# One core, two hybrid layers: the second layer's gate blocks one by one over both token halves, residual updates tied to low parts, token loads tied to H loads

## The chip, the cores and the metric

The kernel runs on one core of one Trainium2 chip. The metric is the device time of one execution in microseconds. Three executions of the kernel before took 1627.13 us (median), from 1626.03 to 1629.71. A profiled execution comes beside them; all traces below are of that one.

The engines are called as the profile calls them: PE (TensorE, matmuls), PEld (its weight loads), ACT (ScalarE), DVE (VectorE), POOL (GpSimd) and SP (SyncE, which here only issues DMAs; POOL issues some too). Each engine takes its instructions strictly in the order in which they stand in its queue, so an instruction that waits holds up all that stands behind it.

## The reference

Two layers, 512 tokens, width 2048, all in float32:

```python
def hybrid_layer(x, w_in, w_out, g_pre, g_post, w_alpha, b_alpha, g_gla, g_att, rel_bias):
    h = rmsnorm(x, g_pre)
    z = h @ w_in                                   # 2048 x 7184
    gq, gk, gv, gg, ga, aq, ak, av, ag = split_columns(z)
    log_a = jax.nn.log_sigmoid((ga @ w_alpha + b_alpha)) / GLA_TAU
    o_gla = gla_chunk_causal(gq, gk, gv, log_a)    # 4 heads, state carried over chunks of 64
    o_gla = rmsnorm(o_gla, g_gla) * jax.nn.silu(gg)
    o_att = chunk_band_attention(aq, ak, av, rel_bias)   # 8 heads
    o_att = rmsnorm(o_att, g_att) * jax.nn.silu(ag)
    y = jnp.concatenate([o_gla, o_att], axis=-1) @ w_out  # 2048 x 2048
    return x + rmsnorm(y, g_post)
```

Most of the work is the two projections, `h @ w_in` and `... @ w_out`. The change touches the end of the first layer's output projection, the residual sum behind it, and the first blocks of the second layer's input projection: the two attention gate blocks, `silu(ag)`.

## The kernel before

**Blocks, chunks and jobs.** The columns of `w_in` are cut into 14 blocks of 512 and those of `w_out` into 4. A block is read in 8 chunks of 256 rows, each one tile of 128 partitions x (2 x 512) float32, 512 KB. One chunk's use is a *job* (class `Job`, a list `stream` fixes their order). A job has three parts, each on an engine of its own: `load` (a DMA from SP, L151), `high` (ACT rounds the chunk to a reduced format, `wh`, L202), and `low` (DVE takes what the rounding left, `wl = src - wh`, L211). The token operand is split in the same way, and a product is three matmuls: high x high, high x low, low x high. `ahead()` prepares the jobs some three to five places before PE uses them. Raw chunks live in rings of buffers (`raw` 5, `H` 4, `wh` 4, `wl` 3), so a load waits until an old chunk's low part was taken, and a low part until PE has done with the one three jobs back.

**Two kinds of product.** `std_gemm` (matmuls in L311) multiplies one block plainly: 8 jobs, each with 6 matmuls per token tile of 128 (there are 4 token tiles, two per *half*). `fast_gemm` (L389, L379) takes two blocks together and needs seven products, P1 to P7, of four jobs each, instead of eight; it adds or subtracts chunks on DVE first (`H + r`, L196, for P5, P6 and P4; `H - r`, L198, for P7) and uses sums of token operands ("sa") that are stored in DRAM and read back by SP (L178). In a layer's last pair, W23, the jobs run P1 and P2 in turn, then P5 and P6, P3, P7 and P4.

**Between the layers.** When the third product of W23 is done, the first half of the tokens is finished: `finish_both` (L1366 on) sums the squares, POOL takes the power -1/2 (L431), and DVE adds the scaled projection to the tokens `x`, one instruction per piece (L1386: four of 128x1024 for half 0; two of 128x1024 and four of 128x512 for half 1). Each piece is stored to `x_mid`. `prep_half` then makes the next layer's operand of that half: ACT squares the pieces (L444), DVE sums (L445), POOL takes the power, ACT (L499) and DVE (L501) scale, PE transposes in 32 instructions (L515), ACT evicts (L526), and ACT and DVE split into high and low (L105, L106). Half 1 goes the same way after P4, the last product.

**The second layer's gate blocks.** They are the blocks AG0 and AG1. Before the change they run half by half: AG0 and AG1 over half 0, then AG0 and AG1 over half 1. So each of the 16 chunks is loaded, rounded and subtracted twice, 32 jobs of 12 matmuls, and PE comes to half 1 only after 16 jobs. Layer 0 has no such split.

**What sets the order.** The program is written as Python generators (`tasks`) that are advanced by `pump` while the matmuls are written out; a scheduler of the build then orders each engine's queue. `tc.issue_after(x)` ties an instruction to come behind x in that order. The ties that matter here: a chunk sum in W01 and W23 comes behind the low part two jobs before (`lows[-2]`); P4's chunk sums in layer 0's W23 also come behind half 0's residual additions (`half_adds`); half 1's residual additions come behind low parts of the operand of half 0 (`half_lows`); a token load comes behind the last load of any kind (`last_load`).

Of the kernel before, what the change touches and what calls it, by code (L numbers as in the profile page):

```python
# [33 lines left out]
def hybrid_trunk(  # L34
# [104 lines left out]
    class Job:  # L139
# [14 lines left out]
        def load(self):  # L154
# [4 lines left out]
            top, bottom = (c + 4, c) if end else (c, c + 4)  # L159
            if k == "std":  # L160
                self.raw = self.fetch(rtile("raw", bufs=5), b0, c)
            elif k == "P1":
                p["H", self.c] = self.fetch(rtile("H"), b0, top)
                last_h[0] = last_load[0]
            elif k == "P5":
                p["r", self.c] = self.fetch(rtile("raw", bufs=5), b1, top)
            elif k == "P6":
                p["r", self.c] = self.fetch(rtile("raw", bufs=5), b1, bottom)
            elif k == "P7":
                p["r", self.c] = p.pop(("t", self.c), None) or self.fetch(rtile("raw", bufs=5), b0, top)  # L170
            elif k == "P2" or (k == "P4" and end):
                p["r", self.c] = self.fetch(rtile("raw", bufs=5), b0, bottom)
            sums = (so_d if end else sa_d)[self.l]
            src = sums.get((LEFT.get(k), c))
            if src is not None and b0 != NB_IN and not (k == "P5" and b0 == AV0):
                until(lambda: k == "P4" or (id(sums), LEFT[k], c) in written)
                self.a = rtile("sa", (2, 512), F32R)
                last_load[0] = nc.sync.dma_start(flat(self.a), src).ins  # L178
            if k == "P5" and b0 == W23[0] and self.l == L - 1:
                with tc.issue_after(last_h[0]):  # L180
                    p["t", self.c] = self.fetch(slot(SPARE[self.c], [2, 512]), b0, c + 4)

        def high(self):
# [301 lines left out]
    half_adds, half_lows, half_turns, half_rows = [], [], [], [None]  # L485
# [237 lines left out]
    def layer(l):  # L723
# [595 lines left out]
        def project(o, n, src, gp=None, comb=None, between=None):  # L1319
# [7 lines left out]
            if gp is None and comb is None:  # L1327
                nc.scalar.copy(dst, src)
            j = t2(dtype=BF16)
            nc.scalar.activation(j, y, AF.Square, scale=D ** -0.5, accum_out=ssy[o][:, n : n + 1])  # L1330
# [39 lines left out]
        def finish_both(pair, xs):  # L1370
# [7 lines left out]
            n = 0  # L1378
            for j in range(2):
                t, c0 = 2 * pair + j, 0  # L1380
                for z in xs[j]:
                    wd = z.shape[-1]
                    yt = ys[t, c0 // 1024][:, c0 % 1024 : c0 % 1024 + wd]
                    with tc.issue_after(half_lows[3 + n // 2]) if pair else nullcontext():
                        half_adds.append(
                            nc.vector.scalar_tensor_tensor(  # L1386
                                out=z, in0=yt, scalar=r[:, j : j + 1], in1=z, op0=ALU.mult, op1=ALU.add
                            ).ins
                        )
                    nc.gpsimd.dma_start(x_mid[t * P : (t + 1) * P, c0 : c0 + wd], z)  # L1390
                    n, c0 = n + 1, c0 + wd
                    if c0 % 1024 == 0:
                        yield
# [48 lines left out]
        def residual(k, c):  # L1442
# [5 lines left out]
            elif k in ("P5", "P6") or (k in ("P1", "P2") and c >= 2):  # L1448
# [3 lines left out]
                xs[half].load(last_load[0], 1)  # L1452
# [61 lines left out]
```

## Time and profile before

| | |
|---|---|
| three executions | 1626.03, 1627.13, 1629.71 us |
| the profiled execution, its own time | 1630.47 us |
| its span in the trace | 1628.4 us, 2.1 us lie around it |
| granted PE clock, mean | 0.996 |
| HBM read, written | 377.02 MB, 61.62 MB |
| DMA queue of SP | 375.99 MB, 66.4% of the span on 16 engines |

The page gives the busy time of each engine; with PE at 99% the time is lost only where PE stands still or runs at a lower clock. The trace's timeline gives the start and the length of each instruction, and in brackets how long the engine stood idle before it and what ended that wait. Matmuls of one stream start 0.227 us apart although each one is shown as 0.39 us long, so an idle time in brackets is some 0.16 us less than what PE lost.

### The profile page before, as it was taken

The numbers are of one execution on the slowest core, as the hardware profiler recorded it, in microseconds if no ns is written. First come the engines' busy times: TensorE is split into PE (matmuls) and PEld (weight loads), VectorE is DVE, ScalarE is ACT, GpSimd is POOL, SyncE is SP. The second block draws the span as 40 slices with busy tenths as digits, with TensorE's granted clock in tenths as the row PEclk, the third lists the DMA queues.
The fourth block names the chain that finished last, engine by engine and source line by source line (L and its number), as shares of the span: only waits on it lengthen the run. The fifth ranks groups of instructions, "written<-read, shape, count | busy, mean of one in ns | idle before, by whom it ended". The sixth has DMA issues, their size and how long they took to land.

```text
span 1628.4 us, 24480 instructions
## 1 busy us (share of the span) xinstructions
PE 1605.2 (99%) x8938; PEld 1374.1 (84%) x8938; DVE 1271.8 (78%) x1646; ACT 919.2 (56%) x1507; POOL 128.9 (8%) x192
## 2 busy tenths in 40 slices
PE   9999999999999999999989999999999999999997
PEld 7887999998888778878778889999988887788886
DVE  5987778678677868988878677686786778689887
ACT  7544445566555556665686444456574555565644
POOL 0120000010000010100122000000100100101001
PEclk9999999999999999999999999999999999999999
DMA  9697686785868768697879976866958677686887
GB/s 370 235 386 265 239 296 209 230 304 175 278 215 296 249 227 302 229 345 262 305 240 336 377 248 247 285 229 223 314 212 282 214 282 267 219 305 239 330 301 196
DMA packets 133928, 438.17 MB, mean 269 GB/s; under 512 B 14404, under 2 KB 27204, under 8 KB 133776
## 3 DMA queue, kind: packets, MB, share of 16 engines
q1 hardware_dynamic: 117072, 375.99, 66.4%
q0 software_dynamic: 16160, 59.53, 9.9%
q8 instruction: 71, 1.16, 0.3%
q10 hardware_dynamic: 576, 1.08, 0.2%
q14 instruction: 49, 0.40, 0.1%
HBM read 377.02 MB, written 61.62 MB: 269 GB/s over the span
## 4 chain that ended last, share of the span: by engine, by line
PE 89%; DVE 3%; DMA 3%; issue 2%; ACT 1%; POOL 0%; DVEq 0%; SPq 0%; POOLq 0%; ACTq 0%
PE mm L389 49%; PE mm L379 20%; PE mm L311 8%; PE ax L939 2%; PE ax L389 2%; DMA raw<-in_w_dram 1%; PE ax L1125 1%; PE ax L922 1%; DVE wl L211 1%; PE ax L1097 1%; PE ax L902 1%; PE ax L901 1%; PE ax L900 1%; DMA H<-in_w_dram 1%; DMA S<-g 1%
## 5 line engine op out<-in xcount | busy, mean ns | idle before, releaser
L389 PE MATMUL mm<-wh,sa 128*128 128x512 f32 x1600 | 518.0, 394 | 1.8 <-DMA sa<-S 0.9
L211 DVE TENSOR_TENSOR wl<-H,wh 128x1024 fp32r<-128x1024 f32 x256 | 312.1, 1220 | 98.7 <-PE mm L389 31.7
L202 ACT CAST wh<-H 128x1024 fp32r<-128x1024 f32 x256 | 268.4, 1051 | 212.0 <-PE mm L389 89.7
L389 PEld LDWEIGHTS mm<-wh,sa 128*128 128x128 f32 x1600 | 299.4, 188 | 74.6 <-issue 9.7
L202 ACT CAST wh<-raw 128x1024 fp32r<-128x1024 f32 (+1 forms) x237 | 248.5, 1052 | 200.9 <-PE mm L389 90.4
L211 DVE TENSOR_TENSOR wl<-raw,wh 128x1024 fp32r<-128x1024 f32 (+1 forms) x237 | 287.6, 1216 | 68.1 <-PE mm L389 27.1
L389 PE MATMUL mm<-wl,sa 128*128 128x512 f32 x800 | 312.6, 391 | 0.3 <-DVE wl L211 0.3
L379 PE MATMUL mm<-sa,wh 128*128 128x256 f32 x1280 | 237.4, 285 | 0.0
L389 PE MATMUL mm<-wh,a 128*128 128x512 f32 x640 | 211.5, 394 | 2.1 <-ACT wh L202 2.1
L379 PEld LDWEIGHTS mm<-sa,wh 128*128 128x128 f32 x1280 | 200.2, 191 | 0.3
L379 PE MATMUL mm<-sa,wl 128*128 128x256 f32 x640 | 181.1, 283 | 0.0
L389 PEld LDWEIGHTS mm<-wl,sa 128*128 128x128 f32 x800 | 150.3, 188 | 30.3 <-DVE wl L211 0.7
L196 DVE TENSOR_TENSOR H<-H,raw 128x1024 f32<-128x1024 f32 x144 | 174.9, 1219 | 1.0
L389 PEld LDWEIGHTS mm<-wh,a 128*128 128x128 f32 x640 | 119.3, 188 | 27.7 <-ACT wh L202 2.9
L389 PE MATMUL mm<-wl,a 128*128 128x512 f32 x320 | 125.7, 393 | 0.0
L379 PEld LDWEIGHTS mm<-sa,wl 128*128 128x128 f32 x640 | 122.5, 191 | 0.3 <-DVE wl L211 0.2
L198 DVE TENSOR_TENSOR raw<-H,raw 128x1024 f32<-128x1024 f32 x60 | 73.5, 1224 | 51.9 <-DMA raw<-in_w_dram 51.6
L431 POOL TENSOR_TENSOR sm<-sm,mhalf 128x2 f32<-128x2 f32 (+2 forms) x40 | 53.0, 1324 | 762.5 <-DVE sm L949 459.2
L389 PE MATMUL mm<-wh,g 128*128 128x512 f32 x320 | 101.7, 391 | 1.5 <-ACT ev L341 1.2
L379 PE MATMUL mm<-a,wh 128*128 128x256 f32 x512 | 95.4, 285 | 0.0
L341 ACT COPY ev<-mm 128x512 f32<-128x512 f32 x104 | 60.8, 585 | 60.6 <-PE mm L389 43.9
L217 DVE TENSOR_TENSOR H<-H,raw 128x1024 f32<-128x1024 f32 x48 | 58.7, 1224 | 38.2 <-DMA raw<-in_w_dram 38.1
(247 smaller groups left out, 2316.2 us busy)
## 6 DMA issues: line engine op xcount, KB each, us to landing
raw<-in_w_dram SPq DMA_DIRECT2D x315, 512.0 KB, 5.2
sa<-S SPq DMA_DIRECT2D x184, 512.0 KB, 4.4
H<-in_w_dram SPq DMA_DIRECT2D x64, 512.0 KB, 5.1
sa<-A SPq DMA_DIRECT2D x48, 512.0 KB, 5.8
S<-g POOLq DMA_DIRECT2D x32, 512.0 KB, 9.6
sa<-oS SPq DMA_DIRECT2D x32, 512.0 KB, 5.5
oS<-g POOLq DMA_DIRECT2D x16, 512.0 KB, 4.5
oS<-sa POOLq DMA_DIRECT2D x16, 512.0 KB, 5.7
```

The source lines that it names most:

```text
L196: nc.vector.tensor_tensor(out=h, in0=h, in1=r, op=ALU.add)
L198: nc.vector.tensor_tensor(out=r, in0=h, in1=r, op=ALU.subtract)
L202: last_cast[0] = nc.scalar.copy(self.wh[:, z, :], src[:, z, :]).ins
L211: last_low[0] = nc.vector.tensor_tensor(out=self.wl[:, z, :], in0=self.src[:, z, :], in1=self.wh[:, z, :].bitcast(F32), op=ALU.subtract).ins
L217: nc.vector.tensor_tensor(out=h, in0=h, in1=self.src, op=ALU.add)
L311: nc.tensor.matmul(pss[o], a(part, kk, o) if callable(a) else a[:, part, t], rhs[:, kk, :], start=(i == 0 and kk == 0 and m == 0), stop=(i ...
L341: nc.scalar.copy(e, src[t])
L379: nc.tensor.matmul(dst, lhs[:, kk, f], a[:, part, tok], start=(fresh and kk == 0 and m == 0 and ft % 2 == 0), stop=(c == 3 and kk == 1 and ...
L389: last_mm[0] = nc.tensor.matmul(out_ps[t], a[:, part, tok], rhs[:, kk, :], start=(fresh and kk == 0 and m == 0), stop=(c == 3 and kk == 1 ...
L431: nc.gpsimd.tensor_tensor(out=out_r, in0=v, in1=mhalf[:, : v.shape[-1]], op=ALU.pow)
L900: nc.tensor.matmul(ps[:, :n], self.qh[:, t], self.kh[:, :n], start=True, stop=False)
L939: nc.tensor.matmul(o, self.pt[i][:, j * P : (j + 1) * P], av[hd // 4, j // 2][:, j % 2, (hd % 4) * P : (hd % 4 + 1) * P], start=(j == 0), ...
```

## The change

The change does five things.

1. The gate blocks of layer 1 run AG0 over half 0, AG0 over half 1, then AG1 over all four token tiles: 24 jobs instead of 32. AG1's jobs have 24 matmuls each. The number of matmuls stays. PE comes to half 1 after 8 jobs.
2. In layer 0's W23 (`mid`), the second chunk of the P7 jobs is loaded at P6, into the slots `a110` to `a113` of the first half's operands, and no longer into the ring `raw`. The loads of "sa" are tied behind the last H load there.
3. The tie of P4's chunk sums to half 0's residual additions is gone. Half 1's additions are tied to the last low part of a weight chunk (`last_low`) and the generator pauses after each.
4. In W01, P4's copy out of PSUM and its squares (L1328, L1330) are tied behind the last cast of a weight chunk (`last_cast`).
5. Token loads are tied behind the last H load (`last_h`) instead of the last load.

```diff
@@ Job.load
+            mid = end and b0 == W23[0] and self.l < L - 1
...
-                last_load[0] = nc.sync.dma_start(flat(self.a), src).ins
-            if k == "P5" and b0 == W23[0] and self.l == L - 1:
+                with tc.issue_after(last_h[0]) if mid else nullcontext():
+                    last_load[0] = nc.sync.dma_start(flat(self.a), src).ins
+            if b0 == W23[0] and k == ("P6" if mid else "P5"):
                 with tc.issue_after(last_h[0]):
-                    p["t", self.c] = self.fetch(slot(SPARE[self.c], [2, 512]), b0, c + 4)
+                    p["t", self.c] = self.fetch(slot(f"a11{self.c}" if mid else SPARE[self.c], [2, 512]), b0, c + 4)
@@ Job.high
-                with ExitStack() as ties:
-                    if self.b0 >= NB_IN:
-                        ties.enter_context(tc.issue_after(lows[-2]))
-                    if k == "P4" and self.l < L - 1 and self.b0 == W23[0]:
-                        ties.enter_context(tc.issue_after(half_adds[3 if self.c else 1]))
+                with tc.issue_after(lows[-2]) if self.b0 >= NB_IN else nullcontext():
@@ stream
-            stream += [Job(l, "std", c, b) for half in range(2) for b in (AG0, AG1) for c in CO]
+            stream += [Job(l, "std", c, AG0) for c in CO]
+            stream += [Job(l, "std", c, AG0) for c in CO]
+            stream += [Job(l, "std", c, AG1) for c in CO]
@@ layer
-            for half in range(2):
-                for q, b in enumerate((AG0, AG1)):
-                    std_gemm(
-                        l, b, (2 * half, 2 * half + 1), CO, operand_in, gate_evac(q), rate=1.3, lag=2 * half * q,
-                    )
-                if half == 0:
-                    tasks.append(token_sums(l))
-                    tasks.append(forget_gate())
+            std_gemm(l, AG0, (0, 1), CO, operand_in, gate_evac(0), rate=1.2)
+            tasks.append(token_sums(l))
+            tasks.append(forget_gate())
+            std_gemm(l, AG0, (2, 3), CO, operand_in, gate_evac(0), rate=0.8)
+            std_gemm(l, AG1, range(NT), CO, operand_in, gate_evac(1), rate=1.3, lag=2)
@@ project
-            if gp is None and comb is None:
-                nc.scalar.copy(dst, src)
             j = t2(dtype=BF16)
-            nc.scalar.activation(j, y, AF.Square, scale=D ** -0.5, accum_out=ssy[o][:, n : n + 1])
+            with tc.issue_after(last_cast[0]) if gp is None and comb is None else nullcontext():
+                if gp is None and comb is None:
+                    nc.scalar.copy(dst, src)
+                nc.scalar.activation(j, y, AF.Square, scale=D ** -0.5, accum_out=ssy[o][:, n : n + 1])
@@ finish_both
-                    with tc.issue_after(half_lows[3 + n // 2]) if pair else nullcontext():
-                        half_adds.append(
-                            nc.vector.scalar_tensor_tensor(
-                                out=z, in0=yt, scalar=r[:, j : j + 1], in1=z, op0=ALU.mult, op1=ALU.add
-                            ).ins
+                    with tc.issue_after(last_low[0]) if pair else nullcontext():
+                        nc.vector.scalar_tensor_tensor(
+                            out=z, in0=yt, scalar=r[:, j : j + 1], in1=z, op0=ALU.mult, op1=ALU.add
                         )
...
-                    if c0 % 1024 == 0:
-                        yield
+                    yield
@@ residual
-                xs[half].load(last_load[0], 1)
+                xs[half].load(last_h[0], 1)
```

Three places show how the queues move. In the rows, `wl` is a low part of a weight chunk, `wh` its high part, `raw` and `H` loaded chunks, `sm` a row factor.

**DVE, the start of P4 in layer 0's W23.** Before, from the low part of the last P7 job on:

```order
L211 TENSOR_TENSOR wl_1504_7774<-raw_1493_7720,wh_1496_7739 128x1024
L1334 TENSOR_TENSOR g1_1442_7478<-t2_1500_7748,t2_1397_7287 128x512
L1373 TENSOR_REDUCE sm_1502_7753<-ssy_1328_6933 128x1
L1386 SCALAR_TENSOR_TENSOR g16_1421_7395<-a122_1326_6929,sm_1503_7754,g16_1421_7395 128x1024
L1386 SCALAR_TENSOR_TENSOR g17_1422_7396<-g0_1439_7472,sm_1503_7754,g17_1422_7396 128x1024
L196 TENSOR_TENSOR H_1373_7189<-H_1373_7189,raw_1497_7741 128x1024
L1386 SCALAR_TENSOR_TENSOR g12_1423_7397<-a123_1329_6935,sm_1503_7754,g12_1423_7397 128x1024
L1386 SCALAR_TENSOR_TENSOR g13_1424_7398<-g1_1442_7478,sm_1503_7754,g13_1424_7398 128x1024
L196 TENSOR_TENSOR H_1387_7241<-H_1387_7241,raw_1506_7779 128x1024
L445 TENSOR_REDUCE sm_1507_7785<-sm_1509_7787 128x1
L211 TENSOR_TENSOR wl_1512_7806<-H_1373_7189,wh_1505_7777 128x1024
```

Now, from the same low part:

```order
L209 TENSOR_TENSOR wl_1504_7774<-a113_1466_7562,wh_1496_7739 128x1024
L194 TENSOR_TENSOR H_1387_7241<-H_1387_7241,raw_1506_7779 128x1024
L1332 TENSOR_TENSOR g1_1444_7482<-t2_1500_7748,t2_1397_7287 128x512
L1371 TENSOR_REDUCE sm_1502_7753<-ssy_1328_6933 128x1
L209 TENSOR_TENSOR wl_1512_7806<-H_1373_7189,wh_1505_7777 128x1024
L194 TENSOR_TENSOR H_1393_7277<-H_1393_7277,raw_1514_7811 128x1024
L1382 SCALAR_TENSOR_TENSOR g16_1421_7395<-a122_1326_6929,sm_1503_7754,g16_1421_7395 128x1024
L1382 SCALAR_TENSOR_TENSOR g17_1422_7396<-g0_1441_7476,sm_1503_7754,g17_1422_7396 128x1024
L1382 SCALAR_TENSOR_TENSOR g12_1423_7397<-a123_1329_6935,sm_1503_7754,g12_1423_7397 128x1024
L1382 SCALAR_TENSOR_TENSOR g13_1424_7398<-g1_1444_7482,sm_1503_7754,g13_1424_7398 128x1024
L209 TENSOR_TENSOR wl_1522_7841<-H_1387_7241,wh_1513_7809 128x1024
```

The first P4 job's low part, `wl_1512`, and the chunk sums before it have moved ahead of half 0's four additions; the second job's, `wl_1522`, stands right behind them.

**DVE, between the fourth and the later low parts of AG0, half 0.** Before, half 1's six additions and the low part behind them (`g9`, `g10`, `sg` and `bias` hold half 1's tokens, the `a...` of L106 below are operands of half 0):

```order
L1386 SCALAR_TENSOR_TENSOR g9_1449_7506<-g8_1377_7197,sm_1574_8055,g9_1449_7506 128x1024
L1386 SCALAR_TENSOR_TENSOR g10_1450_7507<-g2_1538_7903,sm_1574_8055,g10_1450_7507 128x1024
L1386 SCALAR_TENSOR_TENSOR sg_1451_7508<-g11_1380_7203,sm_1574_8055,sg_1451_7508 128x512
L1386 SCALAR_TENSOR_TENSOR sg_1452_7509<-g11_1380_7203,sm_1574_8055,sg_1452_7509 128x512
L1386 SCALAR_TENSOR_TENSOR bias_1453_7510<-g3_1541_7909,sm_1574_8055,bias_1453_7510 128x512
L1386 SCALAR_TENSOR_TENSOR bias_1454_7511<-g3_1541_7909,sm_1574_8055,bias_1454_7511 128x512
L211 TENSOR_TENSOR wl_1578_8087<-raw_1567_8037,wh_1576_8067 128x1024
```

Now:

```order
L1382 SCALAR_TENSOR_TENSOR g9_1451_7510<-g8_1377_7197,sm_1574_8055,g9_1451_7510 128x1024
L1382 SCALAR_TENSOR_TENSOR g10_1452_7511<-g2_1538_7903,sm_1574_8055,g10_1452_7511 128x1024
L209 TENSOR_TENSOR wl_1578_8087<-raw_1567_8037,wh_1576_8067 128x1024
L1382 SCALAR_TENSOR_TENSOR sg_1453_7512<-g11_1380_7203,sm_1574_8055,sg_1453_7512 128x512
L1382 SCALAR_TENSOR_TENSOR sg_1454_7513<-g11_1380_7203,sm_1574_8055,sg_1454_7513 128x512
L106 TENSOR_TENSOR a112_1548_7933<-H_1547_7930,a112_1548_7933 128x512
L209 TENSOR_TENSOR wl_1581_8109<-raw_1577_8069,wh_1579_8089 128x1024
L1382 SCALAR_TENSOR_TENSOR bias_1455_7514<-g3_1541_7909,sm_1574_8055,bias_1455_7514 128x512
L1382 SCALAR_TENSOR_TENSOR bias_1456_7515<-g3_1541_7909,sm_1574_8055,bias_1456_7515 128x512
L106 TENSOR_TENSOR a122_1550_7943<-H_1547_7930,a122_1550_7943 128x512
```

All six additions stood ahead of the fifth low part, `wl_1578`; now two stand ahead of it, two ahead of the sixth, `wl_1581`, and two ahead of the seventh.

**PE, behind the transposes of half 1** (`ax` are the tiles in PSUM into which they go; `cst` holds the identity; `a110` is an operand of half 0, `g8` one of half 1). Before, the last transposes of the first batch and what follows:

```order
L515 MATMUL ax_1608_8215<-cst_173,g10_1450_7507 128x128
L515 MATMUL ax_1608_8215<-cst_173,bias_1453_7510 128x128
L515 MATMUL ax_1608_8215<-cst_173,g10_1450_7507 128x128
L515 MATMUL ax_1608_8215<-cst_173,bias_1453_7510 128x128
L311 MATMUL mm_1636_8350<-wl_1613_8249,a110_1527_7856 128x512
L311 MATMUL mm_1636_8350<-wh_1603_8200,a110_1527_7856 128x512 x2
```

Now, the last but one group of transposes and what follows:

```order
L515 MATMUL ax_1626_8308<-cst_173,g9_1451_7510 128x128
L515 MATMUL ax_1626_8308<-cst_173,sg_1454_7513 128x128
L515 MATMUL ax_1626_8308<-cst_173,g9_1451_7510 128x128
L515 MATMUL ax_1626_8308<-cst_173,sg_1454_7513 128x128
L311 MATMUL mm_1631_8330<-wh_1598_8174,g8_1602_8196 128x512
L311 MATMUL mm_1631_8330<-wl_1605_8216,g8_1602_8196 128x512
L311 MATMUL mm_1632_8331<-wh_1598_8174,g8_1602_8196 128x512
```

Before, 16 transposes were followed by matmuls of AG1 on half 0's operands; now 28 are followed by the first matmul on half 1's, and the eight jobs ahead of the transposes are all of AG0 on half 0.

More of the change, by code (lines that the diff above doesn't have):

```diff
@@ L484, in hybrid_trunk @@
     full = {}
-    half_adds, half_lows, half_turns, half_rows = [], [], [], [None]
+    half_lows, half_turns, half_rows = [], [], [None]
     def prep_half(l, half, xs):
@@ L1377, in finish_both @@
             yield
-            n = 0
             for j in range(2):
@@ L1383, in finish_both @@
                     yt = ys[t, c0 // 1024][:, c0 % 1024 : c0 % 1024 + wd]
-                    with tc.issue_after(half_lows[3 + n // 2]) if pair else nullcontext():
-                        half_adds.append(
-                            nc.vector.scalar_tensor_tensor(
-                                out=z, in0=yt, scalar=r[:, j : j + 1], in1=z, op0=ALU.mult, op1=ALU.add
-                            ).ins
+                    with tc.issue_after(last_low[0]) if pair else nullcontext():
+                        nc.vector.scalar_tensor_tensor(
+                            out=z, in0=yt, scalar=r[:, j : j + 1], in1=z, op0=ALU.mult, op1=ALU.add
                         )
                     nc.gpsimd.dma_start(x_mid[t * P : (t + 1) * P, c0 : c0 + wd], z)
-                    n, c0 = n + 1, c0 + wd
-                    if c0 % 1024 == 0:
-                        yield
+                    c0 += wd
+                    yield
         def finish(pair, xs):
```

## The prediction

> **What bounds the kernel now.** I read the page's engine table first, then the list of PE's waits (below, its longest), then the table by windows, and last the timeline of each engine around every wait.
>
> ```profile
> PE 1605.2 (99%) x8938; PEld 1374.1 (84%) x8938; DVE 1271.8 (78%) x1646; ACT 919.2 (56%) x1507; POOL 128.9 (8%) x192
> ```
>
> ```profile
> PE mm L311 <- DVE wl L211: 5.1, 1, 5.1
> ```
>
> ```profile
> 740.00:760.00 20.00, 20.00 (x90) 16.48 (x89) 19.71 (x22) 9.80 (x13) 0.00 (x0) 1.00 0.66 213
> 760.00:780.00 20.00, 20.00 (x90) 16.57 (x89) 13.42 (x13) 9.57 (x12) 0.00 (x0) 1.00 0.99 360
> 880.00:900.00 20.00, 20.00 (x106) 17.06 (x105) 17.41 (x23) 12.13 (x18) 6.63 (x13) 1.00 1.02 402
> ```
>
> PE is busy 99% of the span. The longest wait (columns: total, times, longest) is 5.1 us, the windows (columns: us, PE, PEld, DVE, ACT, POOL busy, clock, DMA share, GB/s) full. So work on ACT, DVE or the queues is worth nothing unless a wait of PE hangs on it. The order of the two programs differs only from the end of layer 0's W01 to layer 1's gate blocks. The waits of that stretch are these:
>
> ```profile
> 726.39 0.39 PE L389 MATMUL mm<-wh,g 128*128 128x512 f32 x1
> 728.30 0.73 PE L389 MATMUL mm<-wh,a 128*128 128x512 f32 x2 [1.52 <-ACT wh L202]
> 729.24 0.73 PE L389 MATMUL ax<-wh,g 128*128 128x512 f32 x2 [0.21 <-ACT wh L202]
> ...
> 781.20 0.47 PE L389 MATMUL mm<-wh,sa 128*128 128x512 f32 x1 [0.41 <-DMA sa<-oS]
> ...
> 794.69 0.39 PE L389 MATMUL mm<-wh,sa 128*128 128x512 f32 x1
> 795.29 0.51 PE L389 MATMUL mm<-wh,g 128*128 128x512 f32 x1 [0.22 <-ACT ev L341]
> 796.82 0.50 PE L389 MATMUL mm<-wh,g 128*128 128x512 f32 x1 [1.02 <-ACT ev L341]
> 798.38 0.50 PE L389 MATMUL mm<-wl,g 128*128 128x512 f32 x1 [1.06 <-DVE wl L211]
> ...
> 823.56 0.84 PE L311 MATMUL mm<-wh,a 128*128 128x512 f32 x3
> 829.51 0.79 PE L311 MATMUL mm<-wl,a 128*128 128x512 f32 x1 [5.12 <-DVE wl L211]
> ```
>
> In a stream the matmuls start 0.227 us apart (three in 0.84 us, the last 0.39 long), a job of 12 takes 2.72. What PE lost at a place is the distance of two starts less 0.227 for each matmul in between.
>
> ```profile
> 800.00:805.00 5.00, 4.90 (x26) 3.91 (x25) 4.39 (x6) 3.14 (x4) 3.30 (x2) 1.00 0.93 315
> 825.00:830.00 5.00, 0.49 (x1) 0.49 (x2) 5.00 (x8) 5.00 (x13) 3.07 (x7) 0.80 0.78 298
> 830.00:835.00 5.00, 5.00 (x13) 3.83 (x13) 4.74 (x12) 2.50 (x9) 1.53 (x1) 0.52 1.00 268
> ```
>
> The long wait costs twice: behind it the granted clock is 0.52 and 13 matmuls fill 5 us. Behind the three waits near 795 to 798, none over 1.1 us, it stays 1.00.
>
> **The change part by part.** *Fewer jobs.* Eight jobs of AG0 and AG1 go: eight casts (1.05 us, row 843.37 below), eight low parts (1.22, row 828.24) and eight loads of 512 KB. They lie under matmuls: the windows there show PE busy all the time (880 to 900: 20.00 of 20). Worth nothing by itself; the cover is the matmuls of AG0 and AG1, whose number stays. AG1's jobs now have 24 matmuls, which makes that cover thicker.
>
> *W01 to W23 (part 4).*
>
> ```profile
> 726.13 0.59 ACT L1328 COPY g<-mm 128x512 f32<-128x512 f32 x1 [4.74 <-PE mm L389]
> ```
>
> ACT copies and squares out of PSUM while W23's first casts stand behind it. PE lost 728.30 - 726.39 - 0.23 = 1.7 and 729.24 - 728.30 - 0.45 = 0.5, together **2.2**. Now the casts stand ahead and their chunks are there: gone. The copies come later; their banks are wanted only by a later product.
>
> *P7's chunks and the token loads (parts 2 and 5).*
>
> ```profile
> 772.66 8.40 DMA sa<-oS
> ```
>
> In the chain of waits this load takes 8.4 us, and PE lost 0.5 at 781.20. It was issued in a stretch where the DMA share is 0.99 (760 to 780). Four chunks of P7 and the token loads move to the lighter stretch before it (0.66): the **0.5** goes.
>
> *P4's start (part 3).*
>
> ```profile
> 795.90 1.22 DVE L196 TENSOR_TENSOR H<-H,raw 128x1024 f32<-128x1024 f32 x1
> 797.04 0.15 DVE L445 TENSOR_REDUCE sm<-sm 128x1 f32<-128x3 f32 x1
> 797.10 1.22 DVE L211 TENSOR_TENSOR wl<-H,wh 128x1024 fp32r<-128x1024 f32 x1
> ```
>
> PE lost 798.38 - 794.69 - 3 x 0.23 = 3.0 to the two waits and another 0.1 in the short one, **3.1**, because P4's first low part stood behind half 0's four additions (1.2 each, as the two at 823.20 below) and the chunk sums (1.14 by starts). Now the first job's low part is ahead of the additions and the second's right behind them. I walk DVE back to back from the end of the third product, E: six sums or low parts of 1.14 (6.8), four instructions on 512 columns of 0.6 (2.4; three take 1.89 at 821.39 below), two reductions of 0.06 (0.1), four additions (4.8), and the second low part (1.2): 15.4. PE wants that one after five jobs and one matmul, E + 13.8. So **1.7** comes back (bounds 0, if an instruction of the walk is done earlier, and the old 3.1).
>
> *AG0 on half 0 (part 3).*
>
> ```profile
> 821.39 1.89 DVE L106 TENSOR_TENSOR a<-H,a 128x512 fp32r<-128x512 f32 x3
> 823.20 2.47 DVE L1386 SCALAR_TENSOR_TENSOR g<-g,sm,g 128x1024 f32<-128x1024 f32 x2
> ...
> 828.24 1.22 DVE L211 TENSOR_TENSOR wl<-raw,wh 128x1024 fp32r<-128x1024 f32 x1
> ```
>
> Six additions (828.24 - 823.20 = 5.0 us) kept the fifth low part from PE. The loss is 829.51 - 823.56 - 3 x 0.227 = 5.27, and the 12 matmuls from 829.51 end their job 2.56 late at the lower clock: **7.8**. Two things differ now. First, the additions wait for the sum of squares of P4's two last results, and ACT made the second late:
>
> ```profile
> 819.35 0.70 ACT L1330 ACTIVATE t<-mm 128x512 bf16<-128x512 f32 x1
> ```
>
> Both stood behind evictions of transposes (L526); now they stand ahead of these, the second behind one cast. AG0 began four jobs before 823.8, at 812.9, so the second square can start near 813.9. Second, two additions (2.4) stand ahead of the fifth low part, two (1.3) each ahead of the sixth and the seventh. With 819.35 to 823.20, 3.9, from square to addition, they start at 817.8, and the fifth low part ends 2.4 + 1.2 later, at 821.4. PE wants it at 824.24 (823.56 and three matmuls). The sixth ends at 824.5 (two additions, a lo part of 0.6, itself) and is wanted at 827.0; the seventh at 828.8 (two additions, three lo parts, itself), wanted at 829.7, only 0.9 later. POOL's power lies in that 3.9:
>
> ```profile
> 799.61 2.76 POOL L431 TENSOR_TENSOR sm<-sm,mhalf 128x2 f32<-128x2 f32 x1 [2.80 <-DVE sm L445]
> ...
> 821.56 1.07 POOL L431 TENSOR_TENSOR sm<-sm,mhalf 128x2 f32<-128x2 f32 x1 [2.64 <-DVE sm L1373]
> ```
>
> It took 1.07 then and 2.76 at another time; 1.7 more leaves PE 0.8 short. I take **1.0** (0 to 4: none, or such a loss at each of three low parts with the clock's price). The transposes of half 0, in P4, wait for the same step: **0.7** (0 to 2). At the change from P2 to P6, evictions of P2 (0.6 each) now stand ahead of the first low part of P6: **0.7** for one of them (0 to 1.5 for two with a latency).
>
> *The start of half 1 (part 1).* Before, while half 1's operand was made, PE had AG1 on half 0. Now it has nothing but transposes: 28 of them.
>
> ```profile
> 803.96 2.23 PE L515 MATMUL ax<-cst,g 128*128 128x128 f32 x16
> ```
>
> ```profile
> 842.05 0.60 ACT L727 ACTIVATE t<-mm 128x512 f32<-128x512 f32 x1 [0.98 <-PE mm L311]
> 843.37 1.05 ACT L202 CAST wh<-raw 128x1024 fp32r<-128x1024 f32 x1 [0.71 <-PE mm L311]
> ...
> 847.66 0.68 ACT L105 CAST g<-g 128x512 fp32r<-128x512 f32 x1
> ```
>
> Sixteen start over 1.84 us (0.115 each), 28 take 3.2. The same chain stands in the changed queue: eviction, a cast that waits for PE's last job, eviction, the evictions of the transposes, the first high part. It took 848.34 - 842.05 = 6.3 here from the first eviction, 5.0 from the cast. From the cast, which can start as AG0 on half 0 ends, the wait is 5.0 - 3.2 = 1.8; from the first eviction, 3.1. I take **2.4** (bounds 1 and 3.1 for this order).
>
> Sum: 2.2 + 0.5 + 3.1 + 7.8 = 13.6 go; 1.7 + 1.0 + 0.7 + 0.7 + 2.4 = 6.5 come: 7.1 less, 1630.5 - 7.1 = 1623.4 for the profiled execution. That one is 3.3 above the median of the runs, so **1620.0** there.
>
> **The rivals.**
>
> *The clock falls at half 1's start.* From the end of AG0's half 0 PE does no ordinary matmul for 3.2 + 2.4 = 5.6 us. For it: the one stall of like length, 5.3, brought 0.52. Against it: that one was pure idleness, this is mixed with transposes. Price: the 2.6 us of above, so 1622.6. The Trainium skill, "TensorE: Matmul & The Clock Gate", Part 1, has the clock halve after about one idle window of 3.4 us that runs free, and warns of gaps over 3 us; the 5.3 and the 1.0 us waits of this trace agree. Its Part 4 says that transposes do not count as PE activity in the same way, which no row here shows; by it this rival would be the forecast, at 1622.6.
>
> *Crowded DMA earlier.* What moves out of 760 to 780 falls into 740 to 760, together with half 0's tokens. If a chunk lands there as late as that `sa` (8.4 us for a usual 4 to 5), PE waits some 4: 1624.0. Against it: 0.66 leaves a third free.
>
> *Slower: half 1's operand comes no earlier than now.* The split buys time for DVE, not for half 1. Its additions, which stood in a row, are now spread between low parts, and its squares, power, scaling and transposes follow. If its first high part is ready only at 848.3, as now, the gain upstream is lost in the wait. Between the end of AG0's half 0 (the first bank's eviction at 842.05 and six matmuls, 843.4) and 848.3 PE before did 16 transposes and 3.1 us of AG1, of which the 12 transposes more that it has now give back 1.4. So it is 1.7 behind, and 2.6 for a clock that then surely falls: 4.3 slower, 1631.4. My walk has that part ready at 839.0: four more jobs (10.9) behind 824.2 and the 1.0 end AG0's half 0 at 836.1, less the 2.7 gained ahead of it (2.2 + 0.5 + 1.4 - 0.7 - 0.7) 833.4, and 5.6 of transposes and wait. With the clock counted the gain of 7.1 is used up at 4.5 later, 843.5: from there on it is slower. For it: POOL's power once more, and a queue of ACT with casts between the squares. Against it: those casts wait for PE jobs done long before.
>
> *Nothing returns.* The walks are pessimistic throughout and only 1.7 comes back: 1615.
>
> **How the numbers follow.** Forecast 0.49, own range 1617 to 1624 (half of the bounds of each term); clock 0.20; DMA 0.08; late operand 0.19; nothing returns 0.04. A measurement of this kernel can tell 0.2%, 3.25 us, so faster means under 1623.9. Faster: 0.44 of the forecast, 0.04, 0.12 of the clock, 0.02 of the DMA: 0.62. Same: 0.05, 0.08, 0.06 and 0.03 of the late operand: 0.22. Slower: 0.16. Range 1616 to 1630, which leaves out most of the late operand and the best case.
>
> **What would show it.** Right: no wait between W01 and W23 nor for `sa`; one wait of 1 to 2 us at the second P4 job's low part; in AG0's half 0 no wait over 1 us and clock 1.00; at the first matmul on `g8` short waits of 2 to 3 us together, released by ACT's L526 and L105, and clock 1.00 behind them. A clock near 0.5 there speaks for the second case, a wait on a DMA between 740 and 780 for the third, over 5 us at `g8` for the fourth. Wrong would be: a wait that stands where none is listed, above all in AG1 or the attention behind it, whose order did not change.

## The result and the profile after

| | before | changed |
|---|---|---|
| median of 5 executions | 1629.71 us (1626.03 to 1631.51) | 1619.31 us (1618.95 to 1620.84) |
| ratio | | 0.9942, 95% interval 0.9926 to 0.9958 |
| profiled execution, its own time | 1630.47 us | 1619.31 us |
| its span | 1628.4 us | 1617.5 us |

The changed kernel is faster by 0.58%, some 9.4 us (0.42 to 0.74%, 7 to 12 us). Line numbers in it are a little lower behind the edits: low parts are L209, high parts L200, the residual additions L1382.

What is left of PE's waits in the changed kernel (line and releaser; us in total, times, longest):

```profile
PE mm L389 <- DVE wl L209: 1.5, 2, 1.2
...
PE ax L515 <- ACT g L499: 0.4, 1, 0.4
PE ax L515 <- DVE g L501: 0.4, 1, 0.4
PE mm L311 <- ACT g L105: 0.2, 1, 0.2
```

The wait of 5.1 us on a low part is gone, and so is that of 0.4 on `sa` at 781. (Two more on `sa`, at 152 and 156 us in the trace before, are also absent; nothing changed there, so that is chance.) The list doesn't name what PE loses in steps under 0.2 us, so the start of half 1 is read from PE's timeline, here with P4's start in the changed kernel:

```profile
793.74 0.63 PE L389 MATMUL mm<-wh,g 128*128 128x512 f32 x2
795.55 0.50 PE L389 MATMUL mm<-wl,g 128*128 128x512 f32 x1 [1.18 <-DVE wl L209]
...
829.52 0.39 PE L311 MATMUL mm<-wh,a 128*128 128x512 f32 x1
829.79 0.30 PE L515 MATMUL ax<-cst,g 128*128 128x128 f32 x1
830.46 0.52 PE L515 MATMUL ax<-cst,g 128*128 128x128 f32 x3 [0.36 <-DVE g L501]
...
834.85 0.50 PE L311 MATMUL mm<-wh,g 128*128 128x512 f32 x1 [0.21 <-ACT g L105]
```

At P4, 795.55 - 793.74 less two matmuls (0.45): 1.36 us lost. At half 1, 834.85 - 829.52 less one matmul and 28 transposes of 0.11 (3.08): 2.0 lost. The windows there (us; PE, PEld, DVE, ACT, POOL busy; clock; DMA share; GB/s):

```profile
825.00:830.00 5.00, 5.00 (x23) 3.88 (x21) 4.32 (x6) 3.47 (x7) 2.07 (x2) 1.00 0.97 293
830.00:835.00 5.00, 4.19 (x29) 3.00 (x29) 3.20 (x7) 4.81 (x11) 0.97 (x2) 1.00 1.00 377
```

The clock stays at 1.00 although PE does nothing but 28 transposes for 5 us, with 2 us of waits among them. Before, the two windows from 825 to 835 had 0.80 and 0.52.

The start of the same (k-th) matmul in both traces shows where the 10.9 us of span come from:

```
matmul   before   changed   difference   what lies between
 4000    701.68    700.22      1.46      layer 0, the same order
 4300    772.01    768.52      3.49      W01 to W23
 4380    790.84    786.65      4.19      sa, evictions
 4478    812.87    807.68      5.20      P4's start, half 0's transposes
 4568    841.18    828.39     12.79      AG0 on half 0
 5000    928.60    917.86     10.74      start of half 1
 8900   1609.69   1598.86     10.83      all the rest
```

The first 1.46 us are chance: up to there both kernels run the same order, and the traces of this case lie anywhere from 699.2 to 705.1 at that matmul. So the change brought 9.4 in this pair. At a point between, the orders differ by some instructions, so a single difference is good to a few tenths.

### The profile page after: what moved, and what is told of

It is laid out like the page before. It is cut to its first block, busy times and chain, and to the rows that moved or that the text cites. A ratio compares the mean times of both kernels' runs of the same rounds, so it can differ in the third digit from the quotient of the medians.

```text
span 1617.5 us, 24440 instructions
## 1 busy us (share of the span) xinstructions
PE 1602.8 (99%) x8938; PEld 1373.0 (85%) x8938; DVE 1263.3 (78%) x1638; ACT 911.1 (56%) x1499; POOL 130.8 (8%) x192
## 4 chain that ended last, share of the span: by engine, by line
PE 94%; DVE 2%; DMA 2%; issue 1%; ACT 1%; DVEq 0%; SPq 0%; ACTq 0%
PE mm L389 52%; PE mm L379 19%; PE mm L311 10%; PE ax L936 2%; PE ax L389 2%; DMA raw<-in_w_dram 1%; PE ax L1122 1%; PE ax L919 1%; PE ax L746 1%; PE ax L1094 1%; DVE wl L209 1%; PE ax L899 1%; PE ax L898 1%; PE ax L897 1%; DMA bias<-in_rel_dram 0%
## 5 line engine op out<-in xcount | busy, mean ns | idle before, releaser
L200 ACT CAST wh<-H 128x1024 fp32r<-128x1024 f32 x256 | 268.5, 1051 | 220.7 <-PE mm L389 88.9
L209 DVE TENSOR_TENSOR wl<-H,wh 128x1024 fp32r<-128x1024 f32 x256 | 312.1, 1220 | 96.8 <-PE mm L389 29.7
L200 ACT CAST wh<-raw 128x1024 fp32r<-128x1024 f32 (+1 forms) x225 | 235.6, 1051 | 199.4 <-PE mm L389 92.4
L209 DVE TENSOR_TENSOR wl<-raw,wh 128x1024 fp32r<-128x1024 f32 (+1 forms) x225 | 272.7, 1215 | 65.0 <-PE mm L389 23.0
L196 DVE TENSOR_TENSOR raw<-H,raw 128x1024 f32<-128x1024 f32 x56 | 68.5, 1224 | 54.3 <-DMA raw<-in_w_dram 54.0
```

The source lines that it names most:

```text
L196: nc.vector.tensor_tensor(out=r, in0=h, in1=r, op=ALU.subtract)
L200: last_cast[0] = nc.scalar.copy(self.wh[:, z, :], src[:, z, :]).ins
L209: last_low[0] = nc.vector.tensor_tensor(out=self.wl[:, z, :], in0=self.src[:, z, :], in1=self.wh[:, z, :].bitcast(F32), op=ALU.subtract).ins
```

## The experiments

Each time stands beside the kernel before on the same chip, whose medians were 1628.3 to 1628.9 us. Each median is one of 5 to 12 executions.

**One part at a time.** `undo1` takes part 1 back in the changed kernel, `only1` makes part 1 alone in the kernel before (the list of jobs, which follows the same order, changes with it):

```diff
-            std_gemm(l, AG0, (0, 1), CO, operand_in, gate_evac(0), rate=1.2)
...
-            std_gemm(l, AG0, (2, 3), CO, operand_in, gate_evac(0), rate=0.8)
-            std_gemm(l, AG1, range(NT), CO, operand_in, gate_evac(1), rate=1.3, lag=2)
+            for half in range(2):
+                for q, b in enumerate((AG0, AG1)):
+                    std_gemm(
+                        l, b, (2 * half, 2 * half + 1), CO, operand_in, gate_evac(q), rate=1.3, lag=2 * half * q,
+                    )
```

> The changed kernel with part 1 alone undone: gate blocks half by half again, 32 jobs. My theory: part 1 itself brings nothing, since the eight jobs lay under matmuls, and it costs the wait at half 1's start (2.0 us in the changed trace). So 1617.3 us, no wait at the first matmul on half 1's operand, and clock 1.00. Rival: the split frees DVE, ACT and the queues where the additions and half 1's operand need them; then undoing it brings new waits in the gate blocks and the time is 1621 or more.

Measured: 1619.47 us, 0.9948 (0.9935 to 0.9960), not to be told from the changed kernel. In the trace the wait at half 1's start is gone, as expected, and matmul 5000 starts 1.7 us earlier, counted from half 0's first job on. But 190 us later PE lost 2.4 us again, at three waits:

```profile
1035.67 0.38 PE L377 MATMUL mm<-sa,wl 128*128 128x256 f32 x1 [0.59 <-DVE wl L209]
1039.07 0.47 PE L377 MATMUL mm<-sa,wh 128*128 128x256 f32 x2 [0.51 <-DMA sa<-S]
1040.09 0.39 PE L377 MATMUL mm<-sa,wl 128*128 128x256 f32 x1 [0.55 <-DVE wl L209]
```

The chain of waits leads from there to loads of chunks, one of 6.5 us, that had each waited for a low part to free a buffer. Part 1 costs what I said, but taking it back did not pay here. The last experiment below comes back to those waits.

> The kernel before with part 1 alone. My theory: every wait of before stays (13.6 us, of it 7.8 at the fifth low part) and the wait at half 1's start comes on top, 2 us: 2 slower than before, some 1631.7 against 1629.7. Rival of the late operand: half 1's operand comes as late as before and PE, now without other work, stands over 5 us at a lower clock: 4 to 5 slower. Rival that fewer jobs are worth something: equal to before or faster.

Measured: 1628.47 us, 1.0003 (0.9991 to 1.0014): equal, where I had expected 2 us slower. The profiled execution lies 3.4 behind that of the kernel before already at the end of W01, by chance of layer 0. From there to matmul 5000 it is 0.6 us faster. The reason stands in PE's timeline of this kernel:

```profile
833.14 0.50 PE L313 MATMUL mm<-wl,a 128*128 128x512 f32 x1 [3.92 <-DVE wl L211]
```

The stall at the fifth low part is there (3.9 us), and after it there is none at half 1's first matmul: while PE stood at the low part, half 1's operand went on. The two waits hang on one chain, so they don't add: in these traces the wait of part 1 appears only where the long stall is gone.

`only3` makes the changes of part 3 alone in the kernel before, `undo3` takes them back in the changed kernel:

```diff
-                with tc.issue_after(lows[-2]) if self.b0 >= NB_IN else nullcontext():
+                    if k == "P4" and self.l < L - 1 and self.b0 == W23[0]:
+                        ties.enter_context(tc.issue_after(half_adds[3 if self.c else 1]))
...
-                    with tc.issue_after(last_low[0]) if pair else nullcontext():
+                    with tc.issue_after(half_lows[3 + n // 2]) if pair else nullcontext():
```

> The kernel before with part 3 alone (ties of P4's chunk sums and of half 1's additions). My theory: the 7.8 us at the fifth low part go and 1.7 of the 3.1 at P4's start: 9.5 faster than before, some 1620.2 against 1629.7, while the 2.2 between W01 and W23 and the wait for sa stay. Rival: the additions fit between low parts only because part 1 or the earlier loads give room; then some wait over 2 us stays in AG0, and the gain is under 6.

Measured: 1621.9 us, 0.9960 (0.9947 to 0.9974), 6.5 us faster than before by the ratio, 1620.2 expected. No wait on a low part in AG0, clock 1.00 throughout. The waits of 1.52 and 0.21 us between W01 and W23 stand where they stood. Part 3 alone removes the long stall.

> The changed kernel with the old ties of part 3. In its queue four additions stand ahead of P4's first low part again, but two, not six, of half 1's ahead of the fifth low part of AG0, and P4's squares stay ahead of the second batch of evictions. My theory: only P4's start loses (3.1 in place of 1.4), AG0 does not: 1621.0. Rival: the old ties bring the 7.8 back as well: 1628 to 1629.

Measured: 1622.14 us, 0.9968 (0.9955 to 0.9980). P4 has its two waits of 1.03 and 1.06 us again, AG0's half 0 runs through. PE's timeline and the window at P4:

```profile
793.38 0.49 PE L393 MATMUL mm<-wh,g 128*128 128x512 f32 x1 [1.03 <-ACT ev L345]
794.94 0.50 PE L393 MATMUL mm<-wl,g 128*128 128x512 f32 x1 [1.06 <-DVE wl L213]
```

```profile
795.00:800.00 5.00, 5.00 (x15) 3.98 (x16) 4.39 (x6) 2.40 (x3) 2.84 (x2) 0.66 0.97 340
```

Behind them the granted clock was 0.50 for 3.4 us (795.6 to 799.0), in which matmuls start 0.43 apart: 8 of them, some 1.6 us lost. `only1` shows the same at 803.1. The kernel before has the same two waits there (`only1`'s order differs from it only later), and its clock stayed at 1.00. So this price comes in some executions only, and with it P4's waits cost more than the 3.1 us read from the trace before. At half 1's start `undo3` loses 0.8 more than the changed kernel. So the fifth low part doesn't need the new ties as such, but an order with P4's squares ahead of the evictions and two additions, not six, ahead of it. Which of the two counts more was not tried apart.

`undo4` takes part 4 back, `undo25` parts 2 and 5:

```diff
-            with tc.issue_after(last_cast[0]) if gp is None and comb is None else nullcontext():
-                if gp is None and comb is None:
-                    nc.scalar.copy(dst, src)
+            if gp is None and comb is None:
+                nc.scalar.copy(dst, src)
```

```diff
-            if b0 == W23[0] and k == ("P6" if mid else "P5"):
+            if k == "P5" and b0 == W23[0] and self.l == L - 1:
...
-                xs[half].load(last_h[0], 1)
+                xs[half].load(last_load[0], 1)
```

> The changed kernel with part 4 undone: P4's copies and squares in W01 stand ahead of W23's first casts again. My theory: the two waits of 2.2 us between W01 and W23 return and nothing else: 1621.5. Rival: with the other loads tied differently the casts' chunks are early enough and PE has slack: no change, 1619.3.

Measured: 1619.27 us, 0.9946 (0.9933 to 0.9958): no change, the rival. PE has no wait between W01 and W23 without part 4 either. SP's queue tells why. Before, and then in `undo4` (start, us, issue, tile<-source):

```profile
707.77 0.33 SPq L178 DMA_DIRECT2D sa<-oS  x1
...
710.49 0.33 SPq L178 DMA_DIRECT2D sa<-oS  x1
710.87 0.42 SPq L459 DMA_DIRECT2D g<-in_x_dram  x1
...
713.21 0.33 SPq L178 DMA_DIRECT2D sa<-oS  x1
...
714.29 0.48 SPq L459 DMA_DIRECT2D g<-in_x_dram  x1
...
715.53 0.40 SPq L151 DMA_DIRECT2D H<-in_w_dram  x1
```

```profile
713.61 0.33 SPq L151 DMA_DIRECT2D H<-in_w_dram  x1
...
720.99 0.82 SPq L180 DMA_DIRECT2D sa<-oS  x2
721.86 0.42 SPq L459 DMA_DIRECT2D g<-in_x_dram  x1
```

Before, three loads of `sa` and two of tokens stood among the loads ahead of W23's first H chunk; with parts 2 and 5 they are issued behind the H chunks. The time of that one chunk from issue to landing, before and in `undo4`:

```profile
DMA to landing us min/median/max: 10.4/10.4/10.4
```

```profile
DMA to landing us min/median/max: 5.6/5.6/5.6
```

So before it landed at 725.9, and its cast stood behind the copies and began at 727.20. In `undo4` it landed at 719.2, and its cast ran at once, ahead of the copies:

```profile
719.32 1.05 ACT L200 CAST wh<-H 128x1024 fp32r<-128x1024 f32 x1 [1.18 <-DMA H<-in_w_dram]
```

> The changed kernel with parts 2 and 5 undone (P7's chunks and the token loads as before). My theory: the 0.5 us wait for sa in W23 returns, 1619.8, which can't be told from the changed kernel in time, only in the trace. Rival: the early chunks are what lets P4's first low part go ahead; then P4's wait grows by over 1 us too.

Measured: 1622.32 us, 0.9964 (0.9951 to 0.9976), about 3 us slower than the changed kernel; I had expected half a microsecond. With part 4 in place the copies are out of the way, but ACT's first cast for W23 now waits for its chunk, which again took 10.4 us to land:

```profile
724.43 1.05 ACT L198 CAST wh<-H 128x1024 fp32r<-128x1024 f32 x1 [4.59 <-DMA H<-in_w_dram]
```

By the starts of the same matmuls 1.0 us of the loss lies there (two PE waits, 0.29 and 0.22, and what follows them), 0.15 at P4 and 1.2 at half 1's start, where a transpose waits 1.2 us for an eviction. So parts 2 and 5 together remove the whole step that I had put down to part 4 (`undo4`), and part 4 without them leaves 1.0 of it. Which of the two parts does it was not tried apart. The wait for `sa`, which I had expected to return, did not: PE runs through there without parts 2 and 5.

**A late operand, and the clock.** Two kernels bring half 1's operand later, one with PE at work on transposes, one with PE idle:

```diff
+            if half and l and ch == 0:
+                for _ in range(48):
+                    nc.tensor.transpose(ps[:, 0:P], piece(xn[0], 0, P), ident)
```

```diff
+                    if half and l and j == 0 and i == 0:
+                        for _ in range(8):
+                            last_row = nc.vector.tensor_scalar(
+                                out=z, in0=z, scalar1=1.0, scalar2=None, op0=ALU.mult
+                            ).ins
```

> The changed kernel with 48 transposes more ahead of half 1's first (of the same tile, overwritten by the right one). PE does no ordinary matmul for some 10 us, but stands still for no more than now. Theory (transposes count as activity for the granted clock): 48 x 0.111 = 5.3 us more, 1624.6, clock 1.00 at the first matmuls on half 1's operand. Rival (they don't count): clock near 0.5 there and 2.6 or more on top, 1627.2 or more.

Measured: 1624.79 us, 0.9983 (0.9974 to 0.9993). PE's timeline and one window of this kernel:

```profile
829.05 0.40 PE L311 MATMUL mm<-wh,a 128*128 128x512 f32 x1
829.28 5.40 PE L514 MATMUL ax<-cst,g 128*128 128x128 f32 x48
...
838.21 0.50 PE L311 MATMUL mm<-wh,g 128*128 128x512 f32 x1 [0.21 <-ACT g L105]
```

```profile
830.00:835.00 5.00, 5.00 (x48) 5.00 (x47) 2.07 (x5) 1.50 (x5) 0.54 (x1) 1.00 1.00 398
```

Nine microseconds without an ordinary matmul, 72 transposes in them (48 added, 24 of half 1), and the clock is 1.00 (also in the next two windows). The span grew by 4.4 us and not by 5.3, since the added transposes filled half of the 2.0 us wait (838.21 - 829.05 - 0.23 - 72 x 0.11 = 1.0 is left).

> The changed kernel with half 1's operand made late: eight multiplications by 1.0 on DVE (0.66 us each, 5.3 together) behind its scaling. PE stands still for some 5.5 us at the end of AG0's half 0, then does the transposes. Theory: the clock falls as behind the 5.3 us stall of before, so 5.3 + 2 to 3 more: 1626.6 to 1627.6, slightly under the kernel before. Rival: the clock holds, since transposes and the late matmuls come soon: 1624.6.

Measured: 1630.18 us, 1.0009 (0.9999 to 1.0018), so no longer faster than before. My delay was too long: two of the eight multiplications stand between other work, and the last ends near 839.9, 8.2 us behind the end of the scaling. The windows and PE's timeline of this kernel:

```profile
830.00:835.00 5.00, 0.00 (x0) 0.00 (x0) 4.64 (x11) 2.25 (x7) 1.00 (x2) 0.83 0.94 337
835.00:840.00 5.00, 0.00 (x0) 0.01 (x1) 4.70 (x10) 0.27 (x2) 0.00 (x0) 0.50 0.22 84
840.00:845.00 5.00, 4.98 (x26) 4.78 (x27) 1.07 (x2) 3.84 (x10) 0.00 (x0) 0.65 0.06 11
```

```profile
840.02 0.44 PE L520 MATMUL ax<-cst,g 128*128 128x128 f32 x1 [10.37 <-DVE g L506]
...
843.61 0.27 PE L520 MATMUL ax<-cst,sg 128*128 128x128 f32 x1
843.72 0.27 PE L520 MATMUL ax<-cst,g 128*128 128x128 f32 x1
```

PE was idle for 10.4 us and the clock fell. The first 16 transposes start 0.21 apart, the following ones 0.11: the clock came back before the first ordinary matmul. An operand 9 us later cost 9.6 us of span. So the slower rival was a real one, with a price of about one for one; the gain is used up 9 us later, not at the 4.5 of the prediction.

**What is left.** `v_tie` ties the cast of the fourth job of AG0's half 1 behind the evictions of half 1's transposes (and writes it out later in the program, which the cut shown here leaves out); `v_split` lets half 0's third and fourth addition wait for P4's second low part; `v_best` does both; `u1_split` is `v_split` with part 1 taken back.

```diff
+                with tc.issue_after(half_acts[-1]) if hasattr(self, "late") else nullcontext():
                     last_cast[0] = nc.scalar.copy(self.wh[:, z, :], src[:, z, :]).ins
```

```diff
+                    while pair == 0 and j and done["low"] < p4 + 2:
+                        yield
-                    with tc.issue_after(last_low[0]) if pair else nullcontext():
+                    with tc.issue_after(last_low[0]) if pair or j else nullcontext():
```

> The changed kernel; the cast of the fourth job of AG0's half 1, which waits for PE's last job on half 0 and stands ahead of the evictions of half 1's transposes, is moved behind them. My theory of the 2.0 us wait at half 1's start: it is ACT's chain of that cast, an eviction, the evictions and the first high part; without the cast (0.95 us by starts) the wait is 0.8 to 1.2 and the time 1618.3. Rival: the transposes or the scaling before them set it, and the wait stays at 2.0.

Measured: 1619.66 us, 0.9941 (0.9926 to 0.9956). In the trace the wait is shorter: 833.44 - 828.75 - 0.23 - 3.08 = 1.4 us for the 2.0 of the changed kernel.

```profile
828.75 0.39 PE L314 MATMUL mm<-wh,a 128*128 128x512 f32 x1
...
833.44 0.50 PE L314 MATMUL mm<-wh,g 128*128 128x512 f32 x1
```

The cast was in the chain, with 0.6 of its 0.95; the rest is evictions. The timed runs can't tell so little.

> The changed kernel with the low part of P4's second job between the second and third of half 0's four additions. My theory: the wait of 1.2 us at P4 goes, since that low part comes 2.4 us earlier; 0.4 to 0.8 of it returns at the transposes of half 0 or at AG0's first operand, whose chain is 1.2 us later: 1618.5. Rival: all of it returns there, 1619.3 or more.

Measured: 1627.82 us, 0.9994 (0.9986 to 1.0003). The wait at P4 only shrank, from 1.18 to 0.72 us, and nearly all that the change had won is lost at the transposes of half 0. PE's, DVE's and ACT's timelines of this kernel:

```profile
805.49 3.86 PE L515 MATMUL ax<-cst,g 128*128 128x128 f32 x16 [6.12 <-ACT g L499]
```

```profile
794.38 1.22 DVE L194 TENSOR_TENSOR H<-H,raw 128x1024 f32<-128x1024 f32 x1
```

```profile
801.02 1.04 ACT L444 ACTIVATE t<-g 128x1024 bf16<-128x1024 f32 x1
...
804.28 2.19 ACT L499 ACTIVATE g<-g,sm 128x1024 f32<-128x1024 f32 x2 [1.09 <-POOL sm L431]
```

DVE was done with the four additions when it began the chunk sum at 794.38. But the build's order put the two last squares behind casts that wait for that sum, and they ran at 801 to 803. The idle 6.1 us also brought the clock to 0.50 in the window from 805 to 810.

> The changed kernel with both: the cast moved behind half 1's evictions, and P4's second low part between the additions. If the two waits are independent, the gains add: some 1617.5 us. Rival: the later half 0 operand makes half 1's later too, and the sum is no better than the better one alone.

Measured: 1625.92 us, 0.9979 (0.9970 to 0.9989): the 6.12 us wait again. In its trace half 1's start loses 0.8 us, in `v_split`'s 1.7, which is the side on which it is faster.

> Part 1 undone (gate blocks half by half) with P4's second low part between the additions. Part 1 undone gave no wait at half 1's start but three waits of 1.65 us in all at 1035 to 1040, 190 us later, where low parts wait for loads. Theory (these are chance of the loads): they are absent here, no wait at half 1, 1616 to 1617. Rival (they come with the half by half order, its later chunks or stored sums): they stand here again, 1618.5 or more.

Measured: 1624.21 us, 0.9971 (0.9961 to 0.9980). The 6.12 us wait is there too, none at half 1, and none at 1035 to 1040. So those of `undo1` don't belong to the half by half order as such. Whether they come in some of its executions only or from its own timing stays open. `u1_split` against `v_split` is one more pair that differs by part 1: taking it back gains 3.6 us in the medians, 2.5 in the spans.

No version was shown to beat the changed kernel.

## Why the prediction was right

Forecast 1620.0 us, measured 1619.31; forecast gain 7.1, measured 9.4 by the ratio and by the traces. The mechanism held, some terms were mis-sized, and one was put down to the wrong part. That the time came within 0.7 us is luck in part: it starts from a median of three executions, 1627.1, while the other sets of the kernel before have 1628.3 to 1629.7. A start 1.2 to 2.6 us too low and a gain 2.3 too small cancel.

- *Fewer jobs, nothing by itself.* Right: with or without part 1 the time is the same (`undo1`, `only1`).
- *W01 to W23, 2.2.* The size is right (both waits gone; 2.0 by the matmuls, since 0.25 came at 755.67), the cause named first is half of it. I gave it to part 4 and only said in passing that the chunks would be there. `undo4` loses nothing, `undo25` 1.0: the first chunk's late landing was the other half, and with the loads on SP in the new order part 4 is not needed.
- *`sa`, 0.5.* The wait is gone, but that parts 2 and 5 removed it is not shown. Of four traces without these parts, `before` and `only1` have it, `only3` and `undo25` don't.
- *P4's start, 3.1 go, 1.7 come.* Measured 1.4 at the wait, and 1.7 with the short steps around it (0.25 at 792.5 to 792.8, 0.1 behind). The walk had the right place, but not the right filling (and its own terms, 15.4 - 13.8, give 1.6), so that the size is right is luck in part: it ran DVE back to back, while DVE stood still for 0.6 us for POOL's power, which took 2.69 there, and other instructions of the walk were done earlier.
- *AG0 on half 0, 7.8 go, 1.0 comes.* All went, none came. DVE in the changed kernel:

```profile
813.64 2.48 DVE L1382 SCALAR_TENSOR_TENSOR g<-g,sm,g 128x1024 f32<-128x1024 f32 x2
816.04 1.22 DVE L209 TENSOR_TENSOR wl<-raw,wh 128x1024 fp32r<-128x1024 f32 x1
...
823.37 1.22 DVE L209 TENSOR_TENSOR wl<-raw,wh 128x1024 fp32r<-128x1024 f32 x1
```

  and PE at its seventh job:

```profile
824.02 0.84 PE L311 MATMUL mm<-wh,a 128*128 128x512 f32 x3
824.70 0.44 PE L311 MATMUL mm<-wl,a 128*128 128x512 f32 x1
```

  The additions start 6.0 us behind AG0's begin (807.68), where I had walked 4.9, because the second square starts 2.2 behind it and not 1.0. The seventh low part ends at 824.6, and PE takes it at 824.70, without a gap: it came with 0.1 us to spare. The sizing was right to leave a loss open; POOL's power took 1.07 again.
- *Transposes of half 0, 0.7:* 0.6 (801.89 - 800.85 less four transposes). *P2 to P6, 0.7:* nothing at the change, 0.25 two jobs later (755.67). That was the other term too many.
- *Start of half 1, 2.4.* Measured 2.0. The chain of waits of the changed kernel, in order of time, is the one I had named, with one link ahead of it:

```profile
824.62 5.47 DMA raw<-in_w_dram
...
830.19 1.05 ACT wh L200
831.24 0.49 ACT t L727
831.73 2.56 ACT g L526 x7
834.29 0.51 ACT g L105
```

  The cast did not wait for PE's last job, as I had said, but for its chunk (issued at 824.62, landed 5.47 later). The length of the chain from the cast on is 4.6, where the profile before had given 5.0.
- *The rivals.* The clock did not fall at half 1 (1.00). (It fell at P4 in two traces that keep the old waits, `undo3` and `only1`, a price that no rival had.) No load between 740 and 780 kept PE waiting, though the DMA share from 740 to 760 rose to 1.03. The late operand did not come: it was ready at 834.8, 4 us ahead of the walk's 839.0: at AG0's begin the trace was 5.2 us ahead of the one before, where I had reckoned 2.7 (1.46 of it is the chance of layer 0), and AG0 lost nothing. `late_idle` shows its price.

## What to carry to other kernels

Read the few places where the bounding engine stands still, and ask of each which chain it hangs on: waits on one chain do not add, and removing the first may uncover the second (`only1` and the changed kernel). Before an engine's order is mended by a tie, look at whether the tile that the waiting instruction needs is there at all: here loads of `sa` and tokens, moved behind the first chunk on SP's queue, did what the tie on ACT was meant to do. And a tie that helps one instruction can push others far back in the order of the build: one low part moved 2.4 us ahead cost 6 us elsewhere (`v_split`).

## What the runs showed of the hardware

Transposes held the granted clock: 72 of them in 9 us without an ordinary matmul, the first 48 without a pause, left it at 1.00 (`late_turns`), and after a pure stall of 10.4 us, with 0.50 granted, 16 of them, in 3.4 us, sufficed to bring their spacing from 0.21 back to 0.11 us (`late_idle`). The Trainium skill, "TensorE: Matmul & The Clock Gate", Part 4, has transposes not count as PE activity in the same way; these 128x128 float32 transposes, which are matmuls against the identity in this trace, did. Whether they run in the transpose mode that the page speaks of, the trace does not show.

The stalls without any work agree with its Part 1: 3.9 us brought 0.50 for 3.4 us (`only1`, 0.88 and 0.78 in its two windows), 5.3 us brought 0.50 for 6.8 (before), and so did 6.1 us (`v_split`). A single wait of 1.2 us left 1.00 (changed kernel). But a stall of that length is not needed: two waits of 1.0 us with one matmul between them halved the clock for 3.4 us in `undo3` and `only1`, and the same two left it at 1.00 in the kernel before.

The power on POOL, the same instruction on two columns, took 0.70 to 2.76 us. At half 0's residual it took 2.69 in the changed kernel and in ten others, and 0.71 in the three with the old tie of P4's sums (before, `only1`, `undo3`); at half 1's scaling it took 1.78 in the changed kernel and 0.71 in `undo4`. What sets it was not looked into.
